# A first load in two halves of 4 KB runs, and PSUM banks taken in groups of two, three and three, in an attention-score kernel

## The chip, the cores and the metric

The kernel runs on one core of one Trainium2 chip. The metric is the device time of one execution in microseconds (us); the median of three executions of the kernel before is 201.54 us. The profile shown here is of one execution whose span, from the first to the last recorded event, is 200.1 us. Engines are named as in the profile: PE is the matrix engine, PEld its weight load, DVE the vector engine, ACT the scalar engine, POOL the GpSimd engine, SP the sync engine, which here only issues DMAs and waits. A DMA is a transfer between the memory of the device (HBM) and the on-chip memory (SBUF); PSUM is where the matrix engine writes, in eight banks of 512 fp32 values per partition.

## The reference

Scores of attention before the softmax: for each of 8 batches and 8 heads, a 512 x 64 query matrix times the transpose of a 512 x 64 key matrix, times a constant.

```python
def setup_inputs():
    batch, heads, seq, dim = 8, 8, 512, 64
    # q and k: random normal, float32, (batch, heads, seq, dim)

def reference(q, k):
    scale = 1.0 / np.sqrt(q.shape[-1])
    return (np.einsum('bhqd,bhkd->bhqk', q, k) * scale).astype(np.float32)
```

The inputs are two tensors of 8.39 MB, the output is one of 67.11 MB. So the output is four fifths of what moves between HBM and the chip.

## The kernel before

The work is cut into 16 groups `g` (`ALL`). A group is two PSUM fillings of 8 rows x 512 keys, `x` = 0 and 1, and ends in one store of 4 MB. The inputs come in 8 loads of 2 MB, one of `k` and one of `q` for each of four units `v`. The engines work in a chain:

- SP issues the loads, and the stores when a group is ready. Three buffers `bigs` serve the loads first and the stores later.
- POOL casts each load from fp32 to bf16, in two halves `s`, and pairs values so that two bf16 can be moved as one fp32.
- DVE turns the cast data with 32 x 32 stream transposes (two for the keys and four for the queries of a pair of groups) into `kT` and `qz`.
- PE multiplies, one matmul per PSUM bank.
- ACT and DVE take the banks, scale them and write them to the store buffer. Before the change they take two banks at a time: of the eight takes of a group ACT has five and DVE three.

The first load is the only one that is split. The other loads have one 16 KB run per partition; the first load has these runs too, but is issued as four loads of 32 partitions each:

```python
k_r = k.rearrange("(v b) (x s h) (m j) d -> v (s h m) (b x) (j d)", b=2, x=2, s=2, j=R)
pss = [nc.alloc_psum_tensor(f"ps{n}", [P, 2, S], f32)[:] for n in range(4)]
# ... cut
def load_part(queue, n):
    dst = xf(0)[:, 0].rearrange("p s c -> p (s c)")[n:P:4]
    return queue.dma_start(out=dst, in_=rows(0, 0)[:, n]).then_inc(parts[n], 16)

for n, queue in enumerate((nc.sync, nc.scalar)):      # before the barrier of all engines
    tc.no_tile_sem_insts.add(load_part(queue, n).ins.name)
tc.close()
tc.compile()

takers = ["act", "dve", "act", "act", "dve", "act", "dve", "act"]
# ... cut
for n in (2, 3):                                       # after the barrier
    load_part(nc.sync, n)
for n in range(1, 2 * (UNITS - 1)):                    # q0, k1, q1, k2, q2
    load(n // 2, n % 2)
nc.sync.sem_inc(sem["next0"], 1)
for x in range(2):                                     # k3, q3
    nc.sync.wait_ge(sem["ready"], 3 + x)
    load(UNITS - 1, x)
for g in range(ALL):
    for who in ("act", "dve"):
        nc.sync.wait_ge(sem[f"{who}{g // 2 % 2}"], share[who] * (g % 2 + 1))
    nc.sync.dma_start(out=out_r[g // 4, g // 2 % 2, g % 2], in_=...).then_inc(store_sems[g % 3], 16)
    for later in ((1, 2) if g == 0 else (g + 2,)):
        # ... cut: wait for the last cast out of this buffer, or for the store that used it before
            nc.sync.sem_inc(sem[f"next{later // 2 % 2}"], 1)
```

The matmul loop waits, at the first matmul of each two banks, for whoever took these banks last; at the second matmul of a group for `next`. Three matmuls of every second group take the counts off the semaphores (`off`), so that they can be used again:

```python
for p in range(PAIRS):
    # ... cut
    for w in range(2):
        if w == 0:
            who = takers[ahead]
            pe.wait_ge(sem[f"{who}{of // 2}"], of % 2 * share[who] + taken[ahead])
        elif p == 0:
            pe.wait_ge(sem[f"next{two}"], r + 1)
        ins = pe.matmul(out=pss[p % 4][:, w, :], lhsT=qz[:, n, i + w], rhs=kT[:, n],
                        start=True, stop=True)
        if w == 0 and r == 1 and p in off:
            ins.then_inc(sem[f"{off[p][0]}{1 - two}"], -off[p][1])
    ins.then_inc(sem["pe"], 1)
```

The last part interleaves, on DVE, the takes with the transposes for the groups to come:

```python
after = {(0, 1): 1, (0, 4): 1, (0, 6): 2, (1, 1): 2}
for pair in range(ALL * PAIRS):
    g, p = divmod(pair, PAIRS)
    # ... cut: wait for PE, then nc.scalar.mul or nc.vector.tensor_scalar over two banks
    for _ in range(after.get((g % 2, p), 0)):
        next(coming, None)
```

Of the kernel before, what the change touches and what calls it, by code (L numbers as in the profile page):

```python
# [5 lines left out]
def kernel(  # L6
# [5 lines left out]
    nc = tc.nc  # L12
    B, H, S, D = q.shape
    scale = 1.0 / (D ** 0.5)
    P = 128
    Q = 32
    UNITS = B // 2
    G = H // 2
    M = P // (2 * H)
    R = S // M  # L20
    J = R // 2
    RO = 8
    U = S // RO
    JJ = J // RO
    PAIRS = RO
    ALL = 2 * B

    f32 = mybir.dt.float32
    bf16 = mybir.dt.bfloat16
    mult = mybir.AluOpType.mult  # L30
# [3 lines left out]
    names = ["ready", "zeroed", "pe", "next0", "next1", "act0", "act1", "dve0", "dve1"]  # L34
    sem = {name: nc.alloc_semaphore(name) for name in names}
    load_sems = [nc.alloc_semaphore(f"load{n}") for n in range(2 * UNITS)]
    parts = [load_sems[0]] + [nc.alloc_semaphore(f"load0_{n}") for n in range(1, 4)]
    store_sems = [nc.alloc_semaphore(f"store{n}") for n in range(3)]

    q_r = q.rearrange("(v b) (x s h) (m j) d -> v (s h m) (b x) (j d)", b=2, x=2, s=2, j=R)
    k_r = k.rearrange("(v b) (x s h) (m j) d -> v (s h m) (b x) (j d)", b=2, x=2, s=2, j=R)
    out_r = out.rearrange("(v b) (x s h) (u i) k -> v s b (h u) x (i k)", b=2, x=2, s=2, i=RO)

    bigs = [nc.alloc_sbuf_tensor(f"big{n}", [P, 2, RO, S], f32)[:] for n in range(3)]
    xb = nc.alloc_sbuf_tensor("xb", [P, 2 * UNITS, J, D, 2], bf16)[:]
    kT = nc.alloc_sbuf_tensor("kT", [P, 2 * G, S], bf16)[:]
    qz = nc.alloc_sbuf_tensor("qz", [P, 2 * G, RO, P], bf16)[:]
    pss = [nc.alloc_psum_tensor(f"ps{n}", [P, 2, S], f32)[:] for n in range(4)]  # L50

    xw = xb.rearrange("p n w d e -> p n (w d e)").bitcast(f32).rearrange(
        "p n (w d) -> p n w d", d=D)
    kw = kT.bitcast(f32)
# [4 lines left out]
    def xf(v):  # L59
        return bigs[(0, 1, 2, 1)[v]].rearrange("p x i k -> p (x i k)").rearrange(  # L60
            "p (x s c) -> p x s c", x=2, s=2)

    def store_buffer(g):
        return bigs[(0, 2, 1)[g % 3]]

    def rows(v, x):
        return (k_r, q_r)[x][v]
# [4 lines left out]

    def load_part(queue, n):
        dst = xf(0)[:, 0].rearrange("p s c -> p (s c)")[n:P:4]
        return queue.dma_start(out=dst, in_=rows(0, 0)[:, n]).then_inc(parts[n], 16)  # L78

    for n, queue in enumerate((nc.sync, nc.scalar)):  # L80
        tc.no_tile_sem_insts.add(load_part(queue, n).ins.name)
    tc.close()
    tc.compile()  # L83

    takers = ["act", "dve", "act", "act", "dve", "act", "dve", "act"]
    share = {who: takers.count(who) for who in ("act", "dve")}
    taken = [takers[:p + 1].count(takers[p]) for p in range(PAIRS)]


    for n in (2, 3):
        load_part(nc.sync, n)
    for n in range(1, 2 * (UNITS - 1)):
        load(n // 2, n % 2)
    nc.sync.sem_inc(sem["next0"], 1)
# [3 lines left out]
# [3 lines that stand above are left out]
        nc.sync.dma_start(out=out_r[g // 4, g // 2 % 2, g % 2],  # L103
                          in_=store_buffer(g).rearrange("p x i k -> p x (i k)")
# [11 lines left out]

    for v in range(UNITS):
        for x in range(2):
            for part in [load_sems[2 * v + x]] if v or x else parts:
                nc.gpsimd.wait_ge(part, 16)  # L120
            for s in range(2):
                src = xf(v)[:, x, s]
                dst = xb[:, 2 * v + x]
                if x == 0:
                    src = src.rearrange("p (w e d) -> p w e d", e=2, d=D)
                    dst = dst[:, s * J // 2:(s + 1) * J // 2].rearrange("p w d e -> p w e d")
                else:
                    src = src.rearrange("p (jj e i d) -> p jj e i d", e=2, i=RO, d=D)
                    dst = dst.rearrange("p (i jj) d e -> p jj e i d", i=RO)[
                        :, s * JJ // 2:(s + 1) * JJ // 2]  # L130
                cast = nc.gpsimd.tensor_copy(out=dst, in_=src)  # L131
            cast.then_inc(sem["ready"], 1)

    pe = nc.tensor
    pe.wait_ge(sem["zeroed"], 2)
    with pe.Fori(0, ALL // 4):
        for t in range(4):
            two, r = divmod(t, 2)  # L140
            off = {1: ("act", 2 * share["act"]), 2: ("dve", 2 * share["dve"]), 3: ("next", 2)}
            for p in range(PAIRS):
                n, i = t * 2 + p // 4, p % 4 * 2
                ahead = (p + 4) % PAIRS
                of = t if p >= 4 else (t + 3) % 4
                for w in range(2):
                    if w == 0:
                        who = takers[ahead]
                        pe.wait_ge(sem[f"{who}{of // 2}"], of % 2 * share[who] + taken[ahead])
                    elif p == 0:  # L150
                        pe.wait_ge(sem[f"next{two}"], r + 1)
                    ins = pe.matmul(out=pss[p % 4][:, w, :], lhsT=qz[:, n, i + w], rhs=kT[:, n],  # L152
                                    start=True, stop=True)
                    if w == 0 and r == 1 and p in off:
                        ins.then_inc(sem[f"{off[p][0]}{1 - two}"], -off[p][1])
                ins.then_inc(sem["pe"], 1)

    def turn_keys(b, y):  # L160
        s = b % 2 * 2 * Q
        return nc.vector.transpose(  # L162
            out=kw[2 * y * Q:2 * (y + 1) * Q, b % 2 * G:(b % 2 + 1) * G].rearrange(
                "d g (m w) -> d w m g", w=J),
            in_=xw[s:s + 2 * Q, b // 2 * 2, :, y * Q:(y + 1) * Q])

    def turn_queries(b, y, h):
        s = (b % 2 * 2 + h) * Q
        d = (2 * y + h) * Q
        return nc.vector.transpose(  # L170
            out=qw[d:d + Q, b % 2 * G:(b % 2 + 1) * G, :, h * Q:(h + 1) * Q].rearrange(
                "d g i (m jj) -> d i jj m g", jj=JJ),
            in_=xw[s:s + Q, b // 2 * 2 + 1, :, y * Q:(y + 1) * Q].rearrange(
                "p (i jj) d -> p i jj d", i=RO))

    def steps(b):
        nc.vector.wait_ge(sem["ready"], b // 2 * 2 + 1)
        yield turn_keys(b, 0)
        yield turn_keys(b, 1)
        nc.vector.wait_ge(sem["ready"], b // 2 * 2 + 2)  # L180
        for y in range(2):
            for h in range(2):
                yield turn_queries(b, y, h)
# [7 lines left out]
    last.then_inc(sem["zeroed"], 1)  # L191


    after = {(0, 1): 1, (0, 4): 1, (0, 6): 2, (1, 1): 2}
    coming = iter(())
    for pair in range(ALL * PAIRS):
        g, p = divmod(pair, PAIRS)
        o = store_buffer(g)[:, p // 4, p % 4 * 2:p % 4 * 2 + 2, :]
        ps = pss[pair % 4]
        if takers[p] == "act":  # L200
            nc.scalar.wait_ge(sem["pe"], pair + 1)
            freed = nc.scalar.mul(out=o, in_=ps, mul=scale)  # L202
        else:
            nc.vector.wait_ge(sem["pe"], pair + 1)
            freed = nc.vector.tensor_scalar(out=o, in0=ps, scalar1=scale, scalar2=None, op0=mult)  # L205
        freed.then_inc(sem[f"{takers[p]}{g // 2 % 2}"], 1)
        if p == 0 and g % 2 == 0 and g // 2 + 1 < 2 * UNITS:
            coming = steps(g // 2 + 1)
        for _ in range(after.get((g % 2, p), 0)):
            next(coming, None)  # L210


# [28 lines left out]
```

## Time and profile before

| what | value |
|---|---|
| time, median of three | 201.54 us |
| span of the profiled execution | 200.1 us |
| bytes read from and written to HBM | 16.78 MB and 67.11 MB |
| mean rate over the span | 419 GB/s |
| busy: DVE / PE / ACT / POOL | 154.9 / 85.8 / 79.5 / 39.0 us |
| matmuls and takes in the program | 256 matmuls, 80 takes by ACT, 48 by DVE |
| first store issued / last store issued | 36.9 us / 177.4 us |

The profile's page has for each engine its busy time and share of the span; a picture of the span in 40 slices of 5 us, where a digit is the busy share in tenths, with the share of the 16 DMA engines and the GB/s they moved; a chain of waits that leads from the last instruction back; and groups of instructions with their mean duration. A group's row gives the line, engine, operation, what it writes and reads, shapes, count, then busy time and the mean of one in ns, then the idle time of the engine before these instructions and what ended most of it. A busy DVE and a busy DMA do not by themselves say which sets the time; that has to be read from when each could have started.

### The profile page before, as it was taken

The numbers are of one execution on the slowest core, as the hardware profiler recorded it, in microseconds if no ns is written. First come the engines' busy times: TensorE is split into PE (matmuls) and PEld (weight loads), VectorE is DVE, ScalarE is ACT, GpSimd is POOL, SyncE is SP. The second block draws the span as 40 slices with busy tenths as digits, with TensorE's granted clock in tenths as the row PEclk, the third lists the DMA queues.
The fourth block names the chain that finished last, engine by engine and source line by source line (L and its number), as shares of the span: only waits on it lengthen the run. The fifth ranks groups of instructions, "written<-read, shape, count | busy, mean of one in ns | idle before, by whom it ended". The sixth has DMA issues, their size and how long they took to land.

```text
span 200.1 us, 839 instructions
## 1 busy us (share of the span) xinstructions
PE 85.8 (43%) x252; PEld 27.5 (14%) x256; DVE 154.9 (77%) x97; ACT 79.5 (40%) x81; POOL 39.0 (19%) x20
## 2 busy tenths in 40 slices
PE   0000056294844483547236822754575357910000
PEld 0000021121211121112112211211121112300000
DVE  3317959997999899999998999899989996830000
ACT  2000027163752485248443843383437345840000
POOL 0199999996000000000000000000000000000000
PEclk9999999757875588587975799696559667995555
DMA  5999999999999999999999999999999999999996
GB/s 213 380 432 419 432 439 436 423 406 439 429 429 429 436 429 431 426 436 436 429 426 431 436 432 429 429 432 432 429 436 429 432 429 429 426 429 426 436 432 265
DMA packets 5554, 83.90 MB, mean 419 GB/s; under 512 B 432, under 2 KB 432, under 8 KB 432
## 3 DMA queue, kind: packets, MB, share of 16 engines
q1 hardware_dynamic: 5504, 83.36, 97.9%
q10 hardware_dynamic: 48, 0.52, 0.7%
q14 instruction: 2, 0.02, 0.0%
HBM read 16.78 MB, written 67.11 MB: 419 GB/s over the span
## 4 chain that ended last, share of the span: by engine, by line
DVE 54%; DMA 11%; POOL 10%; PE 6%; ACT 3%; SPq 2%; issue 1%
DVE qz L170 24%; DVE big L205 19%; DVE kT L162 12%; DMA big<-in_k_dram 11%; POOL xb L131 10%; PE ps L152 6%; ACT big L202 3%; SPq L70 2%; SPq L78 1%; SPq L112 0%
## 5 line engine op out<-in xcount | busy, mean ns | idle before, releaser
L152 PE MATMUL ps<-kT,qz 128*128 128x512 bf16 x252 | 85.8, 496 | 90.4 <-DVE big L205 57.0
L202 ACT ACTIVATE big<-ps 128x1024 f32<-128x1024 f32 x80 | 78.2, 1025 | 95.4 <-PE ps L152 95.4
L170 DVE STREAM_TRANSPOSE qz<-xb 32x1024 f32<-32x1024 f32 x32 | 64.1, 2004 | 1.5 <-POOL xb L131 1.0
L205 DVE TENSOR_SCALAR big<-ps 128x1024 f32<-128x1024 f32 x48 | 57.8, 1219 | 9.3 <-PE ps L152 8.9
L152 PEld LDWEIGHTS ps<-kT,qz 128*128 128x128 bf16 x256 | 27.5, 118 | 148.3 <-issue 71.6
L131 POOL CAST xb<-big 128x2048 bf16<-128x2048 f32 x16 | 38.8, 2472 | 9.0 <-DMA big<-in_k_dram 8.7
L162 DVE STREAM_TRANSPOSE kT<-xb 64x1024 f32<-64x1024 f32 x16 | 31.1, 1944 | 7.6 <-POOL xb L131 7.1
L185 DVE MEMSET qz<- 128x4096 uint32 x1 | 3.5, 3472 | 3.5 <-PEq L83 3.5
L202 ACT ACT_TABLE_LOAD x1 | 1.3, 1283 | 2.6 <-PEq L83 2.6
L225 POOL MEMSET const-float32-0.0<- 128x1 f32 x1 | 0.1, 99 | 0.2 <-issue 0.2
L225 POOL MEMSET const-bfloat16-1.0<- 128x1 bf16 x1 | 0.1, 102 | 0.0
L225 POOL MEMSET const-uint8-127<- 128x1 uint8 x1 | 0.1, 102 | 0.0
L225 POOL MEMSET const-float32-1.0<- 128x1 f32 x1 | 0.1, 99 | 0.0
## 6 DMA issues: line engine op xcount, KB each, us to landing
out_dram<-big SPq DMA_DIRECT2D x16, 4096.0 KB, 15.0
big<-in_q_dram SPq DMA_DIRECT2D x4, 2048.0 KB, 16.0
big<-in_k_dram SPq DMA_DIRECT2D x3, 2048.0 KB, 14.7
big<-in_k_dram SPq DMA_DIRECT2D x3, 512.0 KB, 5.2
big<-in_k_dram ACTq DMA_DIRECT2D x1, 512.0 KB, 5.7
```

The lines of the kernel that those rows point to most:

```text
L70: nc.sync.dma_start(out=xf(v)[:, x].rearrange("p s c -> p (s c)"), in_=rows(v, x)).then_inc(load_sems[2 * v + x], 16)
L78: return queue.dma_start(out=dst, in_=rows(0, 0)[:, n]).then_inc(parts[n], 16)
L131: cast = nc.gpsimd.tensor_copy(out=dst, in_=src)
L152: ins = pe.matmul(out=pss[p % 4][:, w, :], lhsT=qz[:, n, i + w], rhs=kT[:, n], start=True, stop=True)
L162: return nc.vector.transpose(out=kw[2 * y * Q:2 * (y + 1) * Q, b % 2 * G:(b % 2 + 1) * G].rearrange("d g (m w) -> d w m g", w=J), in_=xw[s ...
L170: return nc.vector.transpose(out=qw[d:d + Q, b % 2 * G:(b % 2 + 1) * G, :, h * Q:(h + 1) * Q].rearrange("d g i (m jj) -> d i jj m g", jj=J ...
L185: nc.vector.memset(qz, 0.0).then_inc(sem["zeroed"], 1)
L202: freed = nc.scalar.mul(out=o, in_=ps, mul=scale)
L205: freed = nc.vector.tensor_scalar(out=o, in0=ps, scalar1=scale, scalar2=None, op0=mult)
L225: nc = _bacc.Bacc("TRN2", target_bir_lowering=False, num_devices=1)
```

## The change

It has three parts.

1. The first load of keys is issued as two loads of 1 MB, one on SP's and one on ACT's queue, both before the barrier. Each goes to all 128 partitions, as two runs of 4 KB per partition, and successive partitions lie 4 KB apart in HBM. Each half is what one cast reads, so that the first cast needs only the first half. The meaning of a partition changes for this load, and with it the order in which the key transposes of the first two pairs of groups write (`b < 2`). The aim is to have the first keys in place sooner, with fewer DMA issues.
2. The eight PSUM banks become one tensor that is taken in groups of two (DVE), three (ACT) and three (ACT). So there are fewer and larger takes, and DVE takes a quarter of the banks instead of three eighths. DVE has the transposes in twos after a take.
3. The counts are taken off by matmuls that have no other signal to give (`takes`).

```diff
-    parts = [load_sems[0]] + [nc.alloc_semaphore(f"load0_{n}") for n in range(1, 4)]
+    halves = [load_sems[0], nc.alloc_semaphore("load0b")]
+    k_0 = k.rearrange("(v b) (x s h) (m j) d -> v b (s h m) x (j d)", b=2, x=2, s=2, m=Q)[0]
-    pss = [nc.alloc_psum_tensor(f"ps{n}", [P, 2, S], f32)[:] for n in range(4)]
+    ps = nc.alloc_psum_tensor("ps", [P, RO, S], f32)[:]
... cut
-    for n, queue in enumerate((nc.sync, nc.scalar)):
-        tc.no_tile_sem_insts.add(load_part(queue, n).ins.name)
+    for s, queue in enumerate((nc.sync, nc.scalar)):
+        first_load = queue.dma_start(
+            out=xf(0)[:, 0, s].rearrange("p (x c) -> p x c", x=2), in_=k_0[s]
+        ).then_inc(halves[s], 16)
+        tc.no_tile_sem_insts.add(first_load.ins.name)
... cut
-    takers = ["act", "dve", "act", "act", "dve", "act", "dve", "act"]
-    for n in (2, 3):
-        load_part(nc.sync, n)
+    groups = [(0, 2, "dve"), (2, 3, "act"), (5, 3, "act")]
+    share = {"act": 4, "dve": 2}
... cut
             for s in range(2):
+                if v == x == 0:
+                    nc.gpsimd.wait_ge(halves[s], 16)
... cut
+    takes = {(0, 3): ("next", 2), (1, 3): ("dve", 2 * share["dve"]), (1, 6): ("act", 2 * share["act"])}
+            for x in range(2):
+                before = (2 * t + x - 1) % 8
+                for i in range(RO):
+                    if i in waits:
+                        who, count = waits[i]
+                        pe.wait_ge(sem[f"{who}{before // 4}"], before % 4 * per_half[who] + count)
+                    elif x == 0 and i == 1:
                         pe.wait_ge(sem[f"next{two}"], r + 1)
+                    ins = pe.matmul(out=ps[:, i], lhsT=qz[:, 2 * t + x, i], rhs=kT[:, 2 * t + x],
                                     start=True, stop=True)
+                    if i in signals:
+                        ins.then_inc(sem["pe"], 1)
+                    elif r == 1 and (x, i) in takes:
+                        name, count = takes[x, i]
+                        ins.then_inc(sem[f"{name}{1 - two}"], -count)
... cut
+        if b < 2:
+            out = out.rearrange("d g (m w) -> d g w m", m=Q)
+        else:
+            out = out.rearrange("d g (m w) -> d w m g", w=J)
... cut
-    after = {(0, 1): 1, (0, 4): 1, (0, 6): 2, (1, 1): 2}
+    for g in range(ALL):
+        for x in range(2):
+            for i, rows_, who in groups:
+                ... # take ps[:, i:i + rows_] in one instruction
+            for _ in range(2 if (g % 2, x) != (1, 1) else 0):
+                next(coming, None)
```

More of the change, by code (lines that the diff above doesn't have):

```diff
@@ L24 @@
     JJ = J // RO
-    PAIRS = RO
     ALL = 2 * B
@@ L71, in load @@
                           ).then_inc(load_sems[2 * v + x], 16)
-    def load_part(queue, n):
-        dst = xf(0)[:, 0].rearrange("p s c -> p (s c)")[n:P:4]
-        return queue.dma_start(out=dst, in_=rows(0, 0)[:, n]).then_inc(parts[n], 16)
-    for n, queue in enumerate((nc.sync, nc.scalar)):
-        tc.no_tile_sem_insts.add(load_part(queue, n).ins.name)
+    for s, queue in enumerate((nc.sync, nc.scalar)):
[3 more added lines that the diff above has]
+        tc.no_tile_sem_insts.add(first_load.ins.name)
     tc.close()
     tc.compile()
-    takers = ["act", "dve", "act", "act", "dve", "act", "dve", "act"]
-    share = {who: takers.count(who) for who in ("act", "dve")}
-    taken = [takers[:p + 1].count(takers[p]) for p in range(PAIRS)]
-    for n in (2, 3):
-        load_part(nc.sync, n)
+    groups = [(0, 2, "dve"), (2, 3, "act"), (5, 3, "act")]
+    share = {"act": 4, "dve": 2}
     for n in range(1, 2 * (UNITS - 1)):
@@ L118 @@
         for x in range(2):
-            for part in [load_sems[2 * v + x]] if v or x else parts:
-                nc.gpsimd.wait_ge(part, 16)
+            if v or x:
+                nc.gpsimd.wait_ge(load_sems[2 * v + x], 16)
             for s in range(2):
+                if v == x == 0:
+                    nc.gpsimd.wait_ge(halves[s], 16)
                 src = xf(v)[:, x, s]
@@ L136 @@
     pe = nc.tensor
+    waits, signals = {}, []
+    for i, rows_, who in groups:
+        waits[i] = (who, [w for _, _, w in groups[:groups.index((i, rows_, who)) + 1]].count(who))
+        signals.append(i + rows_ - 1)
+    per_half = {who: count // 2 for who, count in share.items()}
+    takes = {(0, 3): ("next", 2), (1, 3): ("dve", 2 * share["dve"]), (1, 6): ("act", 2 * share["act"])}
     pe.wait_ge(sem["zeroed"], 2)
@@ L140 @@
             two, r = divmod(t, 2)
[L141 to L150, printed above, removed]
+            for x in range(2):
[5 more added lines that the diff above has]
+                    elif x == 0 and i == 1:
                         pe.wait_ge(sem[f"next{two}"], r + 1)
-                    ins = pe.matmul(out=pss[p % 4][:, w, :], lhsT=qz[:, n, i + w], rhs=kT[:, n],
+                    ins = pe.matmul(out=ps[:, i], lhsT=qz[:, 2 * t + x, i], rhs=kT[:, 2 * t + x],
                                     start=True, stop=True)
-                    if w == 0 and r == 1 and p in off:
-                        ins.then_inc(sem[f"{off[p][0]}{1 - two}"], -off[p][1])
-                ins.then_inc(sem["pe"], 1)
+                    if i in signals:
[3 more added lines that the diff above has]
+                        ins.then_inc(sem[f"{name}{1 - two}"], -count)
     def turn_keys(b, y):
         s = b % 2 * 2 * Q
+        out = kw[2 * y * Q:2 * (y + 1) * Q, b % 2 * G:(b % 2 + 1) * G]
+        if b < 2:
+            out = out.rearrange("d g (m w) -> d g w m", m=Q)
+        else:
+            out = out.rearrange("d g (m w) -> d w m g", w=J)
         return nc.vector.transpose(
-            out=kw[2 * y * Q:2 * (y + 1) * Q, b % 2 * G:(b % 2 + 1) * G].rearrange(
-                "d g (m w) -> d w m g", w=J),
+            out=out,
             in_=xw[s:s + 2 * Q, b // 2 * 2, :, y * Q:(y + 1) * Q])
@@ L191 @@
     last.then_inc(sem["zeroed"], 1)
-    after = {(0, 1): 1, (0, 4): 1, (0, 6): 2, (1, 1): 2}
     coming = iter(())
[L196 to L210, printed above, removed]
+    count = 0
+    for g in range(ALL):
+        for x in range(2):
+            for i, rows_, who in groups:
+                count += 1
+                engine = nc.scalar if who == "act" else nc.vector
+                engine.wait_ge(sem["pe"], count)
+                o, src = store_buffer(g)[:, x, i:i + rows_], ps[:, i:i + rows_]
+                if who == "act":
+                    freed = engine.mul(out=o, in_=src, mul=scale)
+                else:
+                    freed = engine.tensor_scalar(out=o, in0=src, scalar1=scale, scalar2=None,
+                                                 op0=mult)
+                freed.then_inc(sem[f"{who}{g // 2 % 2}"], 1)
+            if x == 0 and g % 2 == 0 and g // 2 + 1 < 2 * UNITS:
+                coming = steps(g // 2 + 1)
+            for _ in range(2 if (g % 2, x) != (1, 1) else 0):
+                next(coming, None)
 _INS = ['q', 'k']
```

## The prediction

> **What bounds the kernel now.** I began with the busy shares, where DVE stands out, and then asked whether anything is busier. The picture of the span and the queue totals answer that:
>
> ```profile
> PE 85.8 (43%) x252; PEld 27.5 (14%) x256; DVE 154.9 (77%) x97; ACT 79.5 (40%) x81; POOL 39.0 (19%) x20
> ...
> DVE  3317959997999899999998999899989996830000
> ...
> DMA  5999999999999999999999999999999999999996
> GB/s 213 380 432 419 432 439 436 423 406 439 429 429 429 436 429 431 426 436 436 429 426 431 436 432 429 429 432 432 429 436 429 432 429 429 426 429 426 436 432 265
> ...
> HBM read 16.78 MB, written 67.11 MB: 419 GB/s over the span
> ```
>
> The reader is to see that DVE rests in the last four slices, 20 us, while the DMA row is full from the second slice to the last but one. Next I read the chain of waits, which seems to say something else:
>
> ```profile
> DVE 54%; DMA 11%; POOL 10%; PE 6%; ACT 3%; SPq 2%; issue 1%
> ```
>
> The chain goes back through whatever released each step, and DVE comes up because it is only just fast enough; it does not say that the stores waited for it. To decide I read the windows of the trace (each row: stretch in us, its length, busy us of PE, PEld, DVE, ACT, POOL, the PE clock, the DMA share, GB/s):
>
> ```profile
> 0.00:9.00 9.00, 0.00 (x0) 0.00 (x0) 3.47 (x1) 1.28 (x1) 0.20 (x4) 1.00 0.75 279
> 9.00:198.00 189.00, 85.79 (x252) 27.45 (x256) 151.42 (x96) 78.21 (x80) 38.80 (x16) 0.76 1.01 430
> ```
>
> From 9 to 198 us the DMA engines move 430 GB/s with a share of 1.01. There is no gap for faster compute to fill. All bytes at this rate are 83.9 MB / 430 GB/s = 195.1 us. The first bytes move at about 2.0 us (finer windows have 0 GB/s until 2.0) and the last at about 198.4 us, that is 196.4 us. So of the whole span only about 1.3 us is bandwidth lost while transfers are under way. In 0 to 9 us, 279 x 9 = 2511 KB moved, worth 5.84 us at 430; 7.0 us had gone by since 2.0. So 1.16 us of it is lost there, at the start. The finer windows show where:
>
> ```profile
> 4.50:5.00 0.50, 0.00 (x0) 0.00 (x0) 0.50 (x1) 0.00 (x0) 0.00 (x0) 1.00 0.32 98
> ...
> 6.00:6.50 0.50, 0.00 (x0) 0.00 (x0) 0.50 (x1) 0.00 (x0) 0.00 (x0) 1.00 0.48 197
> ```
>
> And SP's part of the timeline shows why (start, duration, instruction):
>
> ```profile
> 0.73 2.94 SPq L78 DMA_DIRECT2D big<-in_k_dram  x3
> 3.72 1.68 SPq L70 DMA_DIRECT2D big<-in_q_dram  x1
> ```
>
> Only two parts of 512 KB are issued before the barrier. They are 1.05 MB, 2.4 us of transfer, so they run out near 4.5 us. Parts 2 and 3 are issued at 2.54 and 3.09 us, about 1.3 us before their data can flow if the first issue's delay (0.73 to 2.0) is a guide, and the q0 load, issued from 3.72 to 5.40, comes after. Each handover leaves a dip.
>
> Last, the DMA issues, to see how much the stores have in hand:
>
> ```profile
> out_dram<-big SPq DMA_DIRECT2D x16, 4096.0 KB, 15.0
> ```
>
> A store of 4.19 MB takes 9.75 us at 430 GB/s, and lands a median 15.0 us after its issue (the shortest of the 16 takes 13.3). So a store is queued some 3 to 5 us before the engines come to it. Even the first, issued at 36.9 us, finds the 16.78 MB of loads still on their way: these need 39 us from 2.0 us on. And the last is issued at 177.4 us, with 21 us of transfers still to go.
>
> [...] the trace has data only in 16 KB packets (5120 of them would be 83.9 MB), so it is silent on 4 KB. [...]
>
> **The change part by part.**
>
> *First load.* Four issues become two, both at about 0.73 us, and 2.10 MB are in the queues at once: 4.9 us of transfer, from 2.0 to 6.9 us. SP's next issue, q0, moves from 3.72 to about 2.54 (where part 2 stood). Even if it takes 1.68 us again and its data flow 1.3 us later, they are there at 5.5 us, 1.4 us before the keys run out. So both dips should go. Of the 1.16 us lost I count the part after 4.5 us: the windows from 4.5 to 9.0 moved 1491 KB, 3.47 us' worth, so 1.03 us was lost; the rest is start-up that stays. Against it stand 512 packets of 4 KB in place of 128 of 16 KB. I have no duration for them; I allow 5% of 4.9 us, 0.2 us, a guess. Net: -0.8 us.
>
> The casts. Before, the first cast starts at 9.11 us. After, all keys are through by 6.9 us and[...] the cast starts at about 8.5. The q0 cast started 0.16 us after the k casts ended, at 14.08, on q0's landing; that landing should move by the same 0.8 us. So matmuls begin near 26.5 us instead of 27.33. This is worth nothing by itself: the first store is queued behind loads anyway.
>
> *Key transposes in another order.* Four of 16 (1.94 us each) write `64x4x8x32` instead of `64x32x8x4`. Two fall into the 5 us in which DVE waits for the q0 casts, two between takes. If each were twice as long, 4 x 1.94 = 7.8 us of DVE would still be absorbed, by that wait and by the queue ahead of the first stores: 0 us.
>
> *Takes.* Per pair of groups, DVE now does 6 takes x 1.219 + 2 key transposes x 1.944 + 4 query transposes x 2.004 = 19.2 us; two stores need 2 x 9.75 = 19.5 us. After: 4 x 1.219 + 11.9 = 16.8 us. ACT goes from 10 x 1.025 = 10.25 us to 8 x 1.45 = 11.6 us[...]. PE still has 32 matmuls a pair at a spacing of 0.43 us, 13.8 us. All are under 19.5 us. DVE gains 2.4 us per pair, 8 pairs, 19.5 us in all, and every bit lies beside stores that go on at 430 GB/s: 0 us.
>
> *Signals.* Negative counts move to other matmuls. The three per pair of groups cost nothing visible before, and PE waits for banks 57 us in total: 0 us.
>
> Sum: 201.54 - 1.03 + 0.2 = 200.7 us.
>
> **The rivals.**
>
> (a) DVE sets the pace, as 77% and the chain suggest. Then 19.5 us would go, to about 182 us. Against: 182 us would need 83.9 MB / (182 - 3.7 us) = 471 GB/s, above the rate of any slice (at most 439).
>
> (b) Runs of 4 KB are slow. If the first 2.1 MB went at 340 GB/s, they would take 6.2 instead of 4.9 us and give back 1.3 us: about 201.8 us. For: nothing in the trace is that small. Against: only 2.5% of the bytes are concerned.
>
> (c) PSUM becomes the bound. All eight banks are now one filling, and DVE has two transposes between takes, so banks 0 and 1 can stand full for 2 x 1.97 us. A filling then takes 1.22 + 3.94 = 5.16 us on DVE, three of them 15.5; the fourth, without transposes, 1.22 plus a refill of two banks, about 1.1 us (two matmuls at 0.43 and a signal; DVE's waits for PE were 0.85 to 1.34 us). That is 17.8 us a pair against 19.5. If I were off by 2.7 us, each of 8 pairs would run 1 us late: about 208 us, less the lead of 3 to 5 us.
>
> (d) The dips only move: q0's issue is held up longer behind bigger loads, and the queue runs dry at 6.9 us instead. Then the time stays at 201.3 to 201.6 us.
>
> **Range and chances.** The DMA floor, 2.0 + 195.1 + 1.7 us at the end (198.4 to 200.1) + 1.4 us between span and measured time (201.54 - 200.1) = 200.2 us, is what no part of the change can pass unless the rate rises. I put the range from 200.0 to 201.7 us: the floor with 0.2 us of noise below, (b) or (d) above. The closest two of the three times before are 0.16 us apart. Faster by over 2% means under 197.5 us, below the floor: 0.02. Slower by over 2% means over 205.6 us and needs (c): 0.03. Within 2%: 0.95.
>
> **What would show it.** Right: the slices of the DMA row stay full and at 430; the second slice rises from 380 to about 430 GB/s; the windows at 4.5 and 6.0 us have no dip; the first cast starts by 8.6 us; DVE's busy time falls by some 20 us to about 135 and its share to 68%, with the time hardly touched; SP waits longer for stores and less for DVE; stores take longer from issue to landing. Wrong: a DMA slice below 9 in the middle (then (c)); a first slice slower than before, or keys landing after 9 us (then (b)); a dip around 7 us (then (d)); a time under 199.5 us, which would mean that the rate of 430 was not the ceiling I take it for.

## The result and the profile after

The changed kernel takes 200.89 us (median of 6 runs, 200.73 to 200.98); the kernel before, run beside it, takes 201.54 us (median of 5 runs, 201.32 to 202.19; a sixth took 252.01 us, a slow run, and is left out). The ratio is 0.996, with a 95% interval of 0.9943 to 0.9978 (the medians give 0.997): a small gain, clear of the noise.

The page of the kernel after, the rows that answer to those shown of before:

```profile
span 199.6 us, 783 instructions
...
PE 91.5 (46%) x256; PEld 28.7 (14%) x256; DVE 137.8 (69%) x81; ACT 90.1 (45%) x65; POOL 39.0 (20%) x20
...
DVE  4237979993999899899959985997699722220000
...
DMA  6999999999999999999999999999999999999996
GB/s 201 442 433 430 424 433 420 433 407 420 440 437 430 427 424 443 433 428 420 437 437 433 427 420 442 433 430 427 430 440 430 430 424 433 427 430 430 424 430 273
...
DMA 66%; DVE 12%; POOL 5%; PE 3%; ACT 1%; SPq 1%; issue 1%
```

DVE lost 17 us of work and its row now has gaps all along, and the DMA row is as full as it was. The chain of waits has turned over: DMA 66% where it was DVE 54%. That looks like another kernel, and the whole change is worth 0.3 to 0.4% of the time. The chain named DVE before because DVE was just on time (1.95 us more of it per pair of groups give 211.49 us, in a run below); once DVE is early, the same chain goes through the stores.

The second slice of the rate rises from 380 to 442 GB/s. The windows of the kernel after show the start closely (columns as before; the last two are the DMA share and GB/s):

```profile
4.50:5.00 0.50, 0.00 (x0) 0.00 (x0) 0.50 (x1) 0.00 (x0) 0.00 (x0) 1.00 1.02 418
6.00:6.50 0.50, 0.00 (x0) 0.00 (x0) 0.36 (x1) 0.00 (x0) 0.00 (x0) 1.00 0.99 410
0.00:9.00 9.00, 0.00 (x0) 0.00 (x0) 3.47 (x1) 1.28 (x1) 1.05 (x5) 1.00 0.83 311
9.00:198.00 189.00, 91.50 (x256) 28.67 (x256) 134.28 (x80) 88.81 (x64) 37.94 (x16) 0.77 1.00 429
```

The two dips of before, 98 and 197 GB/s, are gone. They were shallower than they looked: the view counts a packet whole in the window where it starts, and half a microsecond is less than a packet of 16 KB takes (mostly 0.61 us). The window next to the first dip of before shows it, with a DMA share far above 1:

```profile
5.00:5.50 0.50, 0.00 (x0) 0.00 (x0) 0.50 (x1) 0.00 (x0) 0.00 (x0) 1.00 1.48 459
```

With the bytes of each packet spread evenly over its duration, the same trace of before has 390 GB/s from 4.5 to 5.0 us, 317 from 5 to 7 us and 386 from 7 to 9 us; the changed kernel has 418, 419 and 426. So the loss at the start is real, but it is a sag and not two holes. Over 0 to 9 us the rate is 311 instead of 279 GB/s: 288 KB more, 0.67 us at 430 GB/s. From 9 us on it is the same (429 against 430). SP's part of the timeline has q0 at 1.96 us instead of 3.72, issued in 0.61 us instead of 1.68:

```profile
0.73 0.43 SPq L77 DMA_DIRECT2D big<-in_k_dram  x1
1.96 0.61 SPq L71 DMA_DIRECT2D big<-in_q_dram  x1
```

And the stores land a median 19.5 us after their issue, where they took 15.0. All but the last are issued earlier and wait longer in the queue; the last is issued at 178.6 us instead of 177.4:

```profile
out_dram<-big SPq DMA_DIRECT2D x16, 4096.0 KB, 19.5
...
big<-in_k_dram SPq DMA_DIRECT2D x1, 1024.0 KB, 7.4
big<-in_k_dram ACTq DMA_DIRECT2D x1, 1024.0 KB, 8.9
```

What SP waits for before it issues a store, or before it frees a buffer for the next group, has changed with it. Before (us in total, times, longest):

```profile
SPq L102 <- DVE big L205: 75.1, 16, 7.5
SPq L112 <- DMA out_dram<-big: 54.0, 13, 5.4
```

After:

```profile
SPq L107 <- DMA out_dram<-big: 108.8, 13, 9.3
...
SPq L97 <- DVE big L212: 16.9, 6, 5.7
```

### The profile page after: what moved, and what is told of

It is laid out like the page before. It is cut to its first block, busy times and chain, and to the rows that moved or that the text cites. A ratio compares the mean times of both kernels' runs of the same rounds, so it can differ in the third digit from the quotient of the medians.

```text
span 199.6 us, 783 instructions
## 1 busy us (share of the span) xinstructions
PE 91.5 (46%) x256; PEld 28.7 (14%) x256; DVE 137.8 (69%) x81; ACT 90.1 (45%) x65; POOL 39.0 (20%) x20
## 4 chain that ended last, share of the span: by engine, by line
DMA 66%; DVE 12%; POOL 5%; PE 3%; ACT 1%; SPq 1%; issue 1%
DMA out_dram<-big 49%; DMA big<-in_q_dram 17%; POOL xb L128 5%; DVE qz L176 4%; DVE kT L169 4%; DVE big L212 4%; PE ps L152 3%; ACT big L210 1%; SPq L71 1%; SPq L107 0%; SPq L97 0%
## 5 line engine op out<-in xcount | busy, mean ns | idle before, releaser
L152 PE MATMUL ps<-kT,qz 128*128 128x512 bf16 x256 | 91.5, 517 | 85.2 <-DVE big L212 31.4
L210 ACT ACTIVATE big<-ps 128x1536 f32<-128x1536 f32 x64 | 88.8, 1450 | 86.5 <-PE ps L152 86.5
L212 DVE TENSOR_SCALAR big<-ps 128x1024 f32<-128x1024 f32 x32 | 39.2, 1225 | 26.4 <-PE ps L152 26.2
L152 PEld LDWEIGHTS ps<-kT,qz 128*128 128x128 bf16 x256 | 28.7, 123 | 147.4 <-issue 57.2
## 6 DMA issues: line engine op xcount, KB each, us to landing
out_dram<-big SPq DMA_DIRECT2D x16, 4096.0 KB, 19.5
```

The lines of the kernel that those rows point to most:

```text
L152: ins = pe.matmul(out=ps[:, i], lhsT=qz[:, 2 * t + x, i], rhs=kT[:, 2 * t + x], start=True, stop=True)
L210: freed = engine.mul(out=o, in_=src, mul=scale)
L212: freed = engine.tensor_scalar(out=o, in0=src, scalar1=scale, scalar2=None, op0=mult)
```

## The experiments

Each ratio is to the kernel before run on the same chip beside it, which took 201.45 to 201.52 us in these runs.

### One half of the change at a time

**The first load alone**: the kernel before with the first load and the key transposes of the change (in the diff shown with the change, the lines on `halves`, `k_0`, `first_load` and `b < 2`; the takers and PSUM tensors stay).

```diff
-    for n, queue in enumerate((nc.sync, nc.scalar)):
-        tc.no_tile_sem_insts.add(load_part(queue, n).ins.name)
+    for s, queue in enumerate((nc.sync, nc.scalar)):
+        first_load = queue.dma_start(out=xf(0)[:, 0, s]..., in_=k_0[s]).then_inc(halves[s], 16)
... cut
-    for n in (2, 3):
-        load_part(nc.sync, n)
```

> The kernel before with only the first load of the change (two halves of 4 KB runs before the barrier, and the key transposes that go with it). Theory L (the whole gain is the two dips of the DMA rate at the start): the time of the changed kernel, 200.9 us, ratio to before 0.994 to 0.998, with 0 to 9 us at about 311 GB/s and DVE still at about 155 us busy. Rival T (the gain comes from DVE and the larger takes): 201.7 us, ratio 1.000.

Measured: 200.99 us, ratio 0.9971 (0.9961 to 0.9980), with 319 GB/s over 0 to 9 us. Theory L holds, rival T falls: the load alone brings what the whole change brings, but for 0.1 us.

**The takes alone**: the changed kernel with the four-part first load of before.

```diff
+    for n, queue in enumerate((nc.sync, nc.scalar)):      # and n = 2, 3 after the barrier
+        tc.no_tile_sem_insts.add(load_part(queue, n).ins.name)
     groups = [(0, 2, "dve"), (2, 3, "act"), (5, 3, "act")]
```

> The changed kernel with the first load of before (four parts, two of them after the barrier): only the PSUM groups of two, three and three and the counts on free matmuls are left of the change. Theory L: 201.6 to 201.8 us, ratio 0.999 to 1.001, with 0 to 9 us at about 279 GB/s as before, although DVE is busy for only about 138 us. Rival T: 200.9 us, ratio 0.996.

Measured: 201.42 us, ratio 0.9991 (0.9978 to 1.0004), with 271 GB/s over 0 to 9 us. The interval takes in 1; its ends stand for 0.4 us faster and 0.1 us slower. Stores land a median 19.4 us after their issue here too, and 14.9 us in the first load alone. So the earlier stores come from the takes, and bring nothing that stands out of the noise.

### How much DVE time was to spare

One more key transpose per pair of groups, 1.95 us of DVE, into a tensor that nothing reads; once in the kernel before, once in the changed one.

```diff
         yield turn_keys(b, 0)
+        turn_spare(b)          # as turn_keys, into a tensor of its own
         yield turn_keys(b, 1)
```

> The kernel before with one more key transpose per pair of groups (1.95 us of DVE, into a spare tensor that nothing reads). It measures how much DVE time the kernel before had left. DVE then needs 19.2 + 1.95 = 21.2 us a pair and two stores need 19.5. My theory (DMA is the bound now and DVE is only just under it): seven pairs in the loop run 1.7 us late each, 12 us, less the 3 to 5 us that stores have in hand: 206 to 211 us. Rival (DVE has slack in the kernel before, so its relief could never have mattered): within 0.5 us of the kernel before.

Measured: 211.49 us, ratio 1.0506 (1.0490 to 1.0522), half a microsecond above the range expected. The page of this run:

```profile
PE 87.5 (42%) x252; PEld 27.5 (13%) x256; DVE 169.1 (81%) x105; ACT 79.3 (38%) x81; POOL 39.0 (19%) x20
...
DMA  6999999999999899979996999799989999799998
GB/s 247 381 422 431 441 422 434 413 428 431 428 434 416 369 425 423 431 325 450 400 409 292 450 400 400 300 450 400 400 350 391 409 400 400 338 413 438 413 450 350
```

This is what it looks like when DVE does set the time: its share goes up by only four points, from 77% to 81%, but every fourth slice or so of the DMA row breaks, to between 292 and 369 GB/s. Stores of groups 5, 7 and 9 are issued at 92.35, 113.99 and 135.58 us, 21.6 us apart; the sum of DVE's work was 21.2.

> The changed kernel with the same additional key transpose per pair of groups. DVE needs 16.8 + 1.95 = 18.7 us a pair and the refill of two banks makes 19.75 of it, against 19.5 for two stores; the lead of the stores covers the rest. My theory (the relief of DVE is real and is slack): 200.8 to 201.2 us, the same as the changed kernel, with DVE busy for about 153 us. Rival (the new groups tie DVE and PE together so that DVE time counts again): over 203 us.

Measured: 200.82 us, ratio 0.9967 (0.9955 to 0.9979), DVE busy for 151.9 us:

```profile
PE 87.6 (44%) x252; PEld 27.4 (14%) x256; DVE 151.9 (76%) x89; ACT 89.8 (45%) x65; POOL 39.0 (20%) x20
...
DMA  5999999999999999999999999999999999999996
```

DVE is at 76%, a point below the kernel before, and the time does not move. So the takes do give what was worked out, at least 1.95 us of DVE per pair of groups, as room and not as time. The same addition costs the kernel before 10 us.

### What in the first load matters

Theory L in its narrow form said that it is enough to queue all of the first load before the barrier. Two runs for that.

```diff
 # changed kernel: one load of 2 MB on SP, in the layout of before
+    first_load = nc.sync.dma_start(out=xf(0)[:, 0]..., in_=rows(0, 0)).then_inc(load_sems[0], 16)
```

> The changed kernel with the first load as one load of 2 MB in 16 KB runs, issued by SP alone before the barrier, and the key transposes of before. Theory L in its narrow form (what counts is that all of the first load is queued before the barrier, not the runs, the halves or the second queue): 200.8 to 201.0 us, ratio 0.996, no dip at 4.5 or 6.0 us, perhaps 0.2 us faster than the changed kernel because the low rate from 2.0 to 3.5 us (25 to 319 GB/s) goes with the small packets. Rival (halves of 4 KB runs over two queues are needed): 201.5 us or more.

Measured: 201.46 us, ratio 0.9994 (0.9982 to 1.0006). Theory L in its narrow form missed; the time is that of its rival, which held the 4 KB halves over two queues to be needed.

```diff
 # kernel before: all four parts before the barrier
-    for n, queue in enumerate((nc.sync, nc.scalar)):
+    for n, queue in enumerate((nc.sync, nc.scalar, nc.sync, nc.scalar)):
```

> The kernel before with its four parts of 32 partitions kept, but all four issued before the barrier, two on each queue. Theory L, narrow form: the dip at 4.5 us goes and q0 comes earlier, 200.9 to 201.1 us, ratio 0.996 to 0.997. Rival (loads of 32 partitions are slow in themselves, whenever they are issued): 201.5 us, ratio 0.999 to 1.000, with dips that stay.

Measured: 201.55 us, ratio 0.9998 (0.9986 to 1.0010). Missed as well, and yet the sag did go: from 4.5 to 9 us neither run has half a microsecond below 415 GB/s, with the bytes of packets spread as above. Windows of the run with one load, the start and the time when the last load ends and the first store begins:

```profile
0.00:9.00 9.00, 0.00 (x0) 0.00 (x0) 3.47 (x1) 1.28 (x1) 0.88 (x5) 1.00 0.79 319
40.00:43.00 3.00, 2.98 (x10) 0.86 (x8) 2.99 (x2) 2.93 (x3) 2.54 (x2) 0.71 0.99 284
```

The same two windows of the changed kernel:

```profile
0.00:9.00 9.00, 0.00 (x0) 0.00 (x0) 3.47 (x1) 1.28 (x1) 1.05 (x5) 1.00 0.83 311
40.00:43.00 3.00, 3.00 (x9) 0.99 (x8) 2.99 (x2) 2.59 (x2) 2.86 (x3) 0.50 0.97 388
```

The start is at least as good, 319 against 311 GB/s; 30 us later the one load gives it back, 284 against 388. The DMA share stays at 0.99: the engines are not idle, their packets take longer. In the trace a packet of 16 KB takes 611 ns nearly everywhere. In the run with one load, 35 packets that start between 39.4 and 41.9 us take 900 to 1312 ns, against 3 in the changed kernel; the trace does not tell packets of q3 from those of the first store. And q3 lands 6.0 to 6.2 us after k3, where k3 lands 4.9 us after q2. In the changed kernel it is 5.0 to 5.1.

So what in the change avoids this? It differs from these two in run length, in the second queue's share, and in the step from partition to partition. In the one load of 16 KB runs, four partitions in a row read from places 512 KB apart, and the next four from 16 KB further on; call this a broken step. In the changed kernel the step is 4 KB throughout, a constant step. Four runs:

```diff
 # changed kernel, 4 KB runs in one load on SP's queue
+    k_0 = k.rearrange("(v b) (x s h) (m j) d -> v (s h m) b x (j d)", b=2, x=2, s=2, m=Q)[0]
+    first_load = nc.sync.dma_start(out=xf(0)[:, 0]..., in_=k_0).then_inc(load_sems[0], 16)
```

> The changed kernel with its two halves of 4 KB runs joined to one load of 2 MB on SP's queue alone, still before the barrier. The first four runs leave this open: with runs of 16 KB before the barrier the start is as fast as in the changed kernel (319 GB/s over 0 to 9 us), but 0.9 us is lost later, when the last load gives way to the first store (262 to 284 GB/s from 40 to 43 us, against 388 in the changed kernel). Theory R (the 4 KB runs are what spares that loss): 200.8 to 201.0 us, ratio 0.997, 40 to 43 us above 370 GB/s. Rival Q (the second queue spares it): 201.4 to 201.6 us, ratio 1.000, 40 to 43 us below 300 GB/s.

Measured: 200.81 us, ratio 0.9959 (0.9942 to 0.9976), 421 GB/s from 40 to 43 us. The second queue is not needed.

```diff
 # the one load of 16 KB runs, reading 2 MB in order
-    in_=rows(0, 0)
+    in_=k[0:2].rearrange("b h (m j) d -> (b h m) (j d)", j=R)
```

> The one load of 2 MB in 16 KB runs before the barrier, but reading the 2 MB in order, so that successive partitions lie a constant 16 KB apart; it gives each partition other keys than the reference wants, and the work is the same. Theory R (run length): 201.4 to 201.6 us, as the one load without the constant step. Rival S (the constant step per partition spares the later loss): 200.8 to 201.0 us.

Measured: 200.73 us, ratio 0.9953 (0.9936 to 0.9970), 393 GB/s from 40 to 43 us. Theory R falls: runs of 16 KB do it too, if they lie a constant step apart. This run and the one load (201.46 us) are the cleanest pair: the same 2 MB, one load, one queue, the same runs, and only another partition for each run. The scores are then not those of the reference, but the work is the same.

```diff
 # four loads of one 4 KB run per partition, at the addresses of before
-        dst = xf(0)[:, 0]...[n:P:4]
-        return queue.dma_start(out=dst, in_=rows(0, 0)[:, n])
+        part = slice(n * 1024, (n + 1) * 1024)
+        dst = xf(0)[:, 0]...[:, part]
+        return queue.dma_start(out=dst, in_=rows(0, 0)[:, :, part])
-    for n, queue in enumerate((nc.sync, nc.scalar)):
+    for n, queue in enumerate((nc.sync, nc.scalar, nc.sync, nc.scalar)):
```

> The kernel before with its first load in four loads of one 4 KB run for each of 128 partitions, at the addresses of before (no constant step), all before the barrier and two on each queue; its twin is the run with four loads of 32 partitions and 16 KB runs on the same queues (201.55 us). Theory R: 200.8 to 201.1 us, with 40 to 43 us above 370 GB/s. Rival S: 201.4 to 201.6 us.

Measured: 201.39 us, ratio 0.9994 (0.9984 to 1.0003). By its time it speaks for rival S, but in part for another reason than S gave: 40 to 43 us is at 388 GB/s, and 0 to 9 us at only 278. It loses at the start what its twin loses later.

> The changed kernel with the first k load on SP and the first q load on ACT, 2 MB each in 16 KB runs, both before the barrier, so that 4 MB are queued at once. Theory R: the start has no dip but the loss comes back at the change from loads to stores, 201.4 to 201.6 us. Rival Q (two queues with deep work spare it): 200.7 to 200.9 us. Either way the first cast starts later than 8.3 us, since the two loads share the engines, and this costs nothing.

The edit, on the one-load kernel:

```diff
+    for x, queue in enumerate((nc.sync, nc.scalar)):
+        first_load = queue.dma_start(out=xf(0)[:, x]..., in_=rows(0, x)).then_inc(load_sems[x], 16)
```

Measured: 201.49 us, ratio 0.9990 (0.9978 to 1.0002), 319 GB/s at the start and 300 from 40 to 43 us. To have 4 MB queued at once did not help. POOL has only its four memsets up to 9 us, so the first cast starts after 9.0 us, where it starts at 8.32 us in the one load; the time does not show it.

One thing goes along with the step in these runs. A single first load with a broken step is issued in 0.63 us and the next issue on SP starts at 2.39 us; with a constant step it is 0.39 to 0.43 us, and 1.90 to 1.94 us. No run separates an earlier queue from the addresses, but the two loads speak against it: there q0 was issued at 0.74 us and the loss stayed.

The last question: does the late loss come from the last load itself?

```diff
 # one-load kernel, q3 reading 2 MB in order; k0 as in before
-    in_=rows(v, x)
+    in_=(q in order, unit 3) if (v, x) == (3, 1) else rows(v, x)
```

> The run with one load of 2 MB in 16 KB runs before the barrier (201.46 us, with 284 GB/s from 40 to 43 us), with the last load, q3, reading 2 MB in order so that partitions lie a constant step apart; some queries are then others than the reference wants. Theory M (the loss comes from the last load's own pattern meeting the first store): it goes, 200.7 to 201.0 us. Theory H (it is set by how the DMA engines were put in step at the start, and lasts): it stays, 201.3 to 201.6 us.

Measured: 201.41 us, ratio 0.9995 (0.9987 to 1.0004), with the loss in its place:

```profile
40.00:43.00 3.00, 3.00 (x8) 0.98 (x7) 2.99 (x2) 2.38 (x3) 2.44 (x2) 0.51 0.96 284
```

Theory M falls. The pattern of the first load decides over a loss that shows 30 us later, in a load that it has nothing to do with: 284 GB/s from 40 to 43 us here, 393 with a constant step in the first load alone. The same edit for the first load and all others:

```diff
-    in_=rows(v, x)        # and rows(0, 0)
+    in_=(k or q in order, unit v)
```

> The same with all eight loads reading 2 MB in order, partitions a constant 16 KB apart; the scores are of other rows than the reference wants. By theory M: 200.6 to 200.9 us. By theory H, where only the first load counts: 200.7 to 200.9 us, as with the first load alone. A time under 200.5 us would mean that the steps of each load cost something by themselves.

Measured: 200.62 us, ratio 0.9958 (0.9944 to 0.9971): as with the first load alone.

All runs side by side, each row from one profiled execution. "Lost" is worked out from the packets of the trace, the bytes of each spread evenly over its duration: the time of the stretch, counted from 2.0 us on, less what its bytes need at 430 GB/s. (The GB/s are those of the view and rougher.) "In order", "last load constant" and "all in order" give partitions other rows than the reference wants. "Broken" and "constant" are said of the whole first load.

| kernel | first load: step, runs | GB/s 0-9 | GB/s 40-43 | lost 0-9 + 40-43, us | lost 0-46, us | time, us |
|---|---|---|---|---|---|---|
| before | broken, 16 KB | 279 | 393 | 1.40 + 0.24 | 1.64 | 201.45 to 201.54 |
| takes alone | broken, 16 KB | 271 | 415 | 1.65 + 0.11 | 1.81 | 201.42 |
| one load | broken, 16 KB | 319 | 284 | 0.81 + 1.07 | 2.10 | 201.46 |
| four parts early | broken, 16 KB | 319 | 262 | 0.67 + 1.17 | 1.92 | 201.55 |
| two loads | broken, 16 KB | 319 | 300 | 0.73 + 0.94 | 2.04 | 201.49 |
| last load constant | broken, 16 KB | 313 | 284 | 0.79 + 1.04 | 1.83 | 201.41 |
| four parts of 4 KB | broken, 4 KB | 278 | 388 | 1.53 + 0.10 | 1.67 | 201.39 |
| changed kernel | constant, 4 KB | 311 | 388 | 0.81 + 0.30 | 1.16 | 200.89 |
| load alone | constant, 4 KB | 319 | 377 | 0.78 + 0.29 | 1.11 | 200.99 |
| one queue | constant, 4 KB | 302 | 421 | 1.00 + 0.20 | 1.23 | 200.81 |
| in order | constant, 16 KB | 306 | 393 | 0.92 + 0.29 | 1.18 | 200.73 |
| all in order | constant, 16 KB | 299 | 393 | 0.98 + 0.24 | 1.19 | 200.62 |

Every kernel with a broken step loses 1.6 to 2.1 us by 46 us, now at the start, now at the change to stores; every kernel with a constant step loses 1.1 to 1.2 us. A constant step inside each load is not enough: before, takes alone and four parts early each split the first load into four that read their 512 KB in order, into every fourth partition, and four parts early still loses 1.17 us at the change to stores. No run that gives the reference's scores beats the changed kernel clearly: the one load of 4 KB runs, which has one DMA less, is at 200.81 us, within the spread of its 200.73 to 200.98. All in order is lower, 200.62 us with four of five runs below 200.65; whether the later loads add something by their step stays open.

## Why the prediction was right, and where it was lucky

**The bound.** 200.7 us was predicted, 200.89 measured. That DMA sets the time and DVE is only just under it holds twice over: without the DVE relief the gain is there (ratio 0.9971), and with the relief alone it is not (0.9991). Rival (a) is out.

**First load.** Predicted: both dips go, -1.03 us, +0.2 us for small packets, -0.8 in all; measured -0.65 us in the medians, nearly all of it in the bytes of the first 9 us (0.67 us by the windows, 0.59 us by the packets). The 1.03 us was read from windows that count a packet where it starts. With the bytes spread over the durations, before loses 0.78 us from 4.5 to 9 us and after 0.08, which is 0.70 us gained; up to 4.5 us after loses 0.1 us more, 0.73 against 0.63. So the first term was too large, since before had only 0.78 us to lose from 4.5 us on; the 0.1 us and the 0.08 us together are about the 0.2 us of the second. q0 came even earlier than I had put it, at 1.96 us instead of 2.54, since the barrier opened sooner: ACT's first instruction behind it, too, starts at 1.97 us instead of 2.55. The issue on SP before it took 0.43 us, but that explains only a part of the 0.6 us, and the rest stays open. Rival (d), dips that move, did not happen: 6.5 to 9 us has no window below 401 GB/s.

The reason was incomplete. The prediction took it that filling the queue before the barrier is the whole matter, since "of the whole span only about 1.3 us is bandwidth lost", and put no term in the sum for the change from loads to stores. In the kernel before that term was 0.24 us. The one load and the four early parts fill the queue too, remove the sag, and then pay 1.1 to 1.2 us there. By the prediction's own working they should have taken about 200.7 us or less; they took 201.5. What makes the difference is the constant step, which the prediction named in no term. The number came out because in this change that term stays at 0.30 us; that was luck.

**4 KB runs.** The 0.2 us were a guess. In the trace of the changed kernel the 512 packets of 4 KB take a median 159 ns and one of 16 KB takes 611, so that 2.1 MB in 4 KB packets need 5.09 us on 16 engines and in 16 KB packets 4.89: 0.2 us more, as guessed. The times show less: with a constant step on one queue, 4 KB took 200.81 and 16 KB 200.73 us, 0.08 us apart, less than either scatters. Rival (b) is out.

**The casts.** Expected at 8.5 us, seen at 8.16; matmuls expected near 26.5 us, seen at 26.6. Two readings were off. The working has all keys through at one time, 6.9 us; that both halves land nearly together was an estimate of mine that no run had shown. They land 1.5 us apart (7.4 and 8.9 us after issues at the same moment). So the first cast, at 8.16 us, does start on the first half alone. And the cast was put 1.6 us behind the last byte, which was an estimate, too: in this trace the last packet of SP's half ends at 7.46 us and that of ACT's at 8.54, 0.7 and 1.1 us before they land. As predicted, an earlier cast is worth nothing in itself: it starts at 8.32 us in the one load, which takes 201.46 us, and at about 8.8 in the one queue, which takes 200.81.

**Key transposes.** The first two take 4.09 us together instead of 3.94, and the time does not show it. This was far below the doubling that I had allowed for.

**Takes.** The row of ACT and the row of DVE in the groups of the kernel after:

```profile
L210 ACT ACTIVATE big<-ps 128x1536 f32<-128x1536 f32 x64 | 88.8, 1450 | 86.5 <-PE ps L152 86.5
...
L212 DVE TENSOR_SCALAR big<-ps 128x1024 f32<-128x1024 f32 x32 | 39.2, 1225 | 26.4 <-PE ps L152 26.2
```

1450 ns is the 1.45 us of the prediction, an estimate of mine that no run had shown: the takes of ACT in the kernel before all have 1024 columns and 1025 ns. DVE's busy time fell to 137.8, not to about 135 us: its groups before add to 156.5 us, but instructions overlap a little and the page had counted 154.9; in the changed kernel the groups add to 138.3 us, only 0.5 us above the page's count. DVE now waits 26 us for PE, where it waited 9: rival (c) shows as a tendency, in room that DVE has. The additional transpose had been expected to use some of the lead of the stores; it cost nothing.

**Signals.** They were run only together with the takes, and the two together move nothing clear of the noise. By themselves they were not tried.

## What to carry to other kernels

A chain of waits that names an engine for half the span can belong to a kernel whose DMA engines never run dry for it, as here with DVE at 54% of the chain and a DMA share of 1.01 from 9 to 198 us: look at the DMA row and at how long stores lie in the queue, and add 2 us to the suspect per period to see whether it counts (here 10 us before the change and nothing after it). In this kernel DMA moves 429 to 430 GB/s from 9 to 198 us, so only the start, the end and the change between loads and stores are left, and they were worth tenths of a per cent. Windows shorter than a few packets say little on the rate: 98 GB/s in half a microsecond here was 390, with packets of 0.61 us. An early gain in bandwidth is only a gain if it is still there at the end (the one load has 319 GB/s at the start, 284 from 40 to 43 us, and no gain in time): compare the bytes of every later stretch before booking it.

## What was not expected of the hardware

The change from loads to stores costs between 0.1 and 1.2 us of DMA time, with the engines busy for most of it (a DMA share of 0.87 to 1.03 from 40 to 43 us) and packets of 16 KB stretched from 611 to as much as 1432 ns (four parts early), and which of these it is was decided by the first load of the program, 30 us earlier. With the first load's partitions at a constant step in HBM it was 0.20 to 0.30 us in all five kernels of the table; without it, it was 0.9 to 1.2 us in the four that had a clean start, and 0.1 to 0.3 us in the three that had lost 1.4 us or more at the start. An order among the 16 DMA engines that is set at the start and lasts, as in theory H, would fit these numbers, but it was not shown: the traces do not say which engine moves which packet. One form of it, packets that start bunched together, does not sort the kernels: around 25 us the 16 packets in flight start within 0.34 us of each other in the one load, but within 0.30 us in the load alone, which loses only 0.29 us there. Why a constant step spares the loss stays open.
